# A float32 indexer on quarters of the array, a longer delay for the top-64, reordered split products and 512-wide last columns in a two-layer transformer trunk

## The chip, the core and the metric

The kernel runs on one core of a Trainium2 chip. The metric is the device time of one execution in microseconds. Engines by their names in the profile: PE is TensorE (matrix products and transposes; PEld is its weight load), DVE is VectorE, ACT is ScalarE, POOL is GpSimd, SP is SyncE, which issues most DMAs.

## What is computed

Two layers on 256 tokens of width 1024, all in float32. In each layer the normalised input is projected once (`w_in`) to seven groups of columns: queries, keys and values of two attentions a and b, and a small indexer (8 query heads of 32, one key head of 32, 8 weights).

```
h = rms_norm(x, g_mix); proj = h @ w_in           # qa ka va | iq ik iw | qb kb vb
dots  = einsum('bqhd,bsd->bqhs', iq, ik) * 32**-0.5
score = einsum('bqhs,bqh->bqs', relu(dots), iw * 8**-0.5)   # chunk-causal mask: chunks of 64
idx   = top_k(score, 64)                          # attention a sees these keys only
out_a = softmax(qa . ka[idx] * 64**-0.5) @ va[idx]          # 8 heads of 64
p     = softmax(qb . kb * 64**-0.5)                          # 4 heads, two maps each
out_b = rms_norm((p[0] - lam * p[1]) @ vb, g_subln) * (1 - lam_init)
x = x + concat(out_a, out_b) @ w_out
h2 = rms_norm(x, g_ffn)
x = x + (silu(h2 @ w_gate) * (h2 @ w_up)) @ w_down           # inner width 2816
```

After the second layer follows one more `rms_norm` with `g_final`. Queries iq, qa, qb and keys ik, ka, kb are turned by rotary angles first.

## The kernel before

Tokens lie in two blocks of 128 (b = 0, 1). Every large product is a split product: activation and weight are each cut into a high part, rounded to the format fp32r, and the rest, so that hi.whi + lo.whi + hi.wlo stands for one float32 product. `mm3` (L195 to L201) issues these three, lines L198, L199 and L200. Contraction runs over k in pieces of 128: 8 for the projections, gate and up, and wo, 22 for down. In one layer TensorE does, in this order, the projections idx, qb, kb, vb, qa, ka, va (2 blocks x 8 k x 3 products of up to 512 columns each), `wo` with the halves mixb (from attention b) and mixa, six column groups j of gate and up (the last one 256 wide), and `down`. In between stand the small works of rotary transposes (`ptq_`), the indexer (`ptx`, `dots`) and the attentions (`lg_` logits, `ppt_` transposed probabilities, `po` outputs).

Weights come in chunks of up to 1 MB by SP's queue into `wraw` (3 buffers). ScalarE rounds them to `whi` (L176), VectorE subtracts to get `wlo` (L177); both have 6 buffers. The first idx projection (L765) alone uses unsplit weights, since it opens the run; the split of its activations is done by `halved` in `startup`.

The indexer: after the rotary step `ixt` is repeated and split into `ixq` and `ixk`, four copies of 32 columns (hi, lo and again, so that one 128-row product contracts hi.hi, hi.lo, lo.hi and lo.lo); ScalarE writes the high parts (L396), VectorE the low ones (L397). Nine transposes per block (`ptx`) put them on partitions. `indexer` then issues eight fp32r products per block (`dots`, two heads per bank), ScalarE applies relu (L447), VectorE adds the weighted scores (L450), and finds the top 64 in eight rounds of MAX (L458) and MATCH_REPLACE (L460), ending in `amask` (L463).

The order on TensorE is written by `Weave`: the large products form the main thread, every other work is a thread that yields a due time (constants such as DIX, DG, DB) and is put between products once the modelled clock has come that far. The order on VectorE and ScalarE is set by the tile scheduler from the order of issue and a priority; the top-64 is issued `with tc.high_priority(offset=-LOWP)`, which puts it behind work issued up to LOWP instructions later.

Of the kernel before, what the change touches and what calls it, by code (L numbers as in the profile page):

```python
# [8 lines left out]
F32 = mybir.dt.float32  # L9
# [8 lines left out]
P = 128  # L18
D = 1024
S = 256  # L20
# [12 lines left out]
LOWP = 100  # L33
DG = 2.0
# [8 lines left out]
DIX = 13.0  # L43
# [66 lines left out]
def tile_hybrid_trunk(ctx, tc, x, xT, w_idx, w_in, w_out, w_gate, w_up, w_down, g_final, rope, out):  # L110
# [12 lines left out]
    NSUB = 1024  # L123
    chunks = []
# [6 lines left out]
    for L in range(DEPTH):  # L131
# [9 lines left out]
        for j in range(6):  # L141
            n = min(512, DFF - j * 512)
            step = 4 if n == 512 else 8
            for nm, w in (("gate", w_gate), ("up", w_up)):
                for a in range(0, KT, step):
                    c = add_chunk(w[L], range(a, a + step), j * 512, n)
                    for k in range(a, a + step):
                        plan[L, nm, j, k] = c
# [8 lines left out]
    def load(c):  # L157
        src, kts, c0, n = chunks[c]
        t = pool.tile([P, len(kts), n], F32, tag="wraw", bufs=3, name=f"wraw{c}")
        if n == NCOL["idx"]:  # L160
            for k in range(0, len(kts), 2):
                nc.sync.dma_start(t[:, k:k + 2], src[:, k:k + 2])
        else:
            nc.sync.dma_start(t, src[kts[0] * P:(kts[-1] + 1) * P, c0:c0 + n].rearrange("(k p) n -> p k n", p=P))
# [215 lines left out]
    def after_proj(L, nm, b, ps):  # L380
        name = f"{nm}{L}{b}"
        r = rstd["mix", L, b]
        if nm == "idx":
# [8 lines left out]
            sk = pool.tile([P, 1, 4, 32], F32R, tag="ixk", bufs=2, name=f"ixk{L}{b}")  # L392
            for st, hd, first, second in ((sq, slice(0, 8), slice(0, 4, 2), slice(1, 4, 2)),
                                          (sk, slice(8, 9), slice(0, 2), slice(2, 4))):
                src = t[:, hd].unsqueeze(2).to_broadcast([P, hd.stop - hd.start, 2, 32])
# [3 lines left out]
            iq = pool.tile([P, 8, P], F32R, tag="iqT", bufs=2, name=f"iqT{L}{b}")  # L399
            if b == 0:  # L400
                T["ik"] = pool.tile([P, S], F32R, tag="ikT", bufs=1, name=f"ikT{L}")
            flat = [v.bitcast(F32).rearrange("p h r d -> p h (r d)") for v in (sq, sk)]
            for g in range(2):
                pt = bank(f"ptx{L}{b}{g}").rearrange("p (k t) -> p k t", k=4)
                for k in range(4):
                    transpose(pt[:, k], flat[0][:, 4 * g + k])
                nc.scalar.copy(iq[:, 4 * g:4 * g + 4], pt)
            pt = bank(f"ptx{L}{b}2")
            transpose(pt[:, :P], flat[1][:, 0])
            nc.scalar.copy(T["ik"][:, b * P:(b + 1) * P], pt[:, :P])  # L410
            T["iq", b] = iq
# [441 lines left out]
```

## Time and profile before

| | |
|---|---|
| median of 3 runs (lowest to highest) | 640.1 us (640.01 to 640.23) |
| profiled execution | 640.0 us |
| its span | 638.2 us |
| PE busy | 628.1 us (98%) |
| PEld busy | 519.5 us (81%) |
| DVE busy | 434.9 us (68%) |
| ACT busy | 360.4 us (56%) |
| chain that ended last | PE 83%, DVE 11%, ACT 2%, issue 2%, DMA 2% |
| granted TensorE clock, tenths in 40 slices | 9 in all but the last, 8 |

The span runs from the first to the last instruction that the profile shows; the execution's own time is 1.8 us longer. Busy shares are averages over the run; by stretches they differ much, and the rows below tell them apart. TensorE's products overlap one another, so what one costs is read from the distance of two starts, not from its duration.

### The profile page before, as it was taken

The page shows a single profiled execution, that of the slowest core. Times are in us where ns is not written, and L with a number is a line of the kernel's source. Part 1 is how long each engine was busy: PE and PEld are TensorE (multiplying, and loading weights), DVE is VectorE, ACT ScalarE, POOL GpSimd, SP SyncE. Part 2 cuts the span into 40 slices and gives each one's busy share as a digit, 9 for nine tenths or more (in the row PEclk, how much of TensorE's full clock was granted, in tenths as well). Part 3 has the DMA queues.
Part 4 walks back from the last instruction along what each step waited for, and adds up shares of the span by engine and source line. Part 5 has one row for each costly group of instructions (what it writes and reads, how often), then busy time and mean ns, then how long its engine had stood idle before and what let it go on. Part 6 is the DMA issues. An engine that isn't in the chain of part 4 may idle for free.

```text
span 638.2 us, 8752 instructions
## 1 busy us (share of the span) xinstructions
PE 628.1 (98%) x3235; PEld 519.5 (81%) x3235; DVE 434.9 (68%) x922; ACT 360.4 (56%) x620; POOL 2.0 (0%) x12
## 2 busy tenths in 40 slices
PE   9999999999999999999999999999999999999996
PEld 5787787788888889888898787878888888898885
DVE  5999997696555456544598999876756555454445
ACT  4868677684454444433477767876744454443322
POOL 1000000000000000000000000000000000000000
PEclk9999999999999999999999999999999999999998
DMA  9873344346655555554277534323755655545611
GB/s 333 283 242 105 120 179 149 132 132 200 196 196 185 192 167 184 198 197 143 66 265 222 174 132 133 132 72 127 258 169 172 196 196 186 195 153 193 198 34 66
DMA packets 49307, 109.64 MB, mean 172 GB/s; under 512 B 1904, under 2 KB 6512, under 8 KB 49264
## 3 DMA queue, kind: packets, MB, share of 16 engines
q1 hardware_dynamic: 48256, 106.96, 50.2%
q10 hardware_dynamic: 1008, 2.12, 0.9%
q8 instruction: 25, 0.41, 0.3%
q14 instruction: 18, 0.15, 0.1%
HBM read 108.02 MB, written 1.05 MB: 171 GB/s over the span
## 4 chain that ended last, share of the span: by engine, by line
PE 83%; DVE 11%; ACT 2%; issue 2%; DMA 2%; ACTq 0%
PE ps_gate L198 6%; PE dn L199 6%; PE dn L198 6%; PE ps_gate L200 6%; PE dn L200 6%; PE ps_gate L199 6%; PE ps_up L200 6%; PE ps_up L198 6%; PE ps_up L199 6%; DVE wlo L177 3%; PE wo L199 2%; PE wo L200 2%; PE wo L198 2%; PE pth L204 2%; DVE topk L460 1%
## 5 line engine op out<-in xcount | busy, mean ns | idle before, releaser
L177 DVE TENSOR_TENSOR wlo<-wraw,whi 128x1024 fp32r<-128x1024 f32 (+1 forms) x200 | 241.5, 1213 | 139.1 <-ACT whi L176 134.5
L176 ACT CAST whi<-wraw 128x1024 fp32r<-128x1024 f32 (+1 forms) x200 | 206.7, 1043 | 153.5 <-PE dn L199 50.0
L198 PE MATMUL ps_gate<-whi,hi_ffn 128*128 128x512 f32 (+1 forms) x192 | 73.6, 383 | 0.0
L198 PE MATMUL dn<-whi,hi_ff 128*128 128x512 f32 (+1 forms) x198 | 73.1, 369 | 0.0
L199 PE MATMUL dn<-whi,lo_ff 128*128 128x512 f32 (+1 forms) x198 | 72.6, 367 | 0.0
L200 PE MATMUL dn<-wlo,hi_ff 128*128 128x512 f32 (+1 forms) x198 | 72.4, 366 | 0.0
L200 PE MATMUL ps_gate<-wlo,hi_ffn 128*128 128x512 f32 (+1 forms) x192 | 71.5, 373 | 0.0
L200 PE MATMUL ps_up<-wlo,hi_ffn 128*128 128x512 f32 (+1 forms) x192 | 71.3, 372 | 0.0
L199 PE MATMUL ps_gate<-whi,lo_ffn 128*128 128x512 f32 (+1 forms) x192 | 71.3, 371 | 0.0
L198 PE MATMUL ps_up<-whi,hi_ffn 128*128 128x512 f32 (+1 forms) x192 | 71.3, 371 | 0.0
L199 PE MATMUL ps_up<-whi,lo_ffn 128*128 128x512 f32 (+1 forms) x192 | 71.3, 371 | 0.0
L200 PEld LDWEIGHTS dn<-wlo,hi_ff 128*128 128x128 f32 x198 | 37.3, 188 | 6.2
L198 PEld LDWEIGHTS dn<-whi,hi_ff 128*128 128x128 f32 x198 | 37.4, 189 | 6.0
L199 PEld LDWEIGHTS dn<-whi,lo_ff 128*128 128x128 f32 x198 | 37.4, 189 | 5.8
L200 PEld LDWEIGHTS ps_gate<-wlo,hi_ffn 128*128 128x128 f32 x192 | 36.1, 188 | 6.6
L200 PEld LDWEIGHTS ps_up<-wlo,hi_ffn 128*128 128x128 f32 x192 | 36.2, 188 | 6.3
L199 PEld LDWEIGHTS ps_up<-whi,lo_ffn 128*128 128x128 f32 x192 | 36.2, 188 | 6.2
L198 PEld LDWEIGHTS ps_up<-whi,hi_ffn 128*128 128x128 f32 x192 | 36.2, 188 | 6.2
L199 PEld LDWEIGHTS ps_gate<-whi,lo_ffn 128*128 128x128 f32 x192 | 36.2, 189 | 5.6
L198 PEld LDWEIGHTS ps_gate<-whi,hi_ffn 128*128 128x128 f32 x192 | 36.2, 188 | 5.5
L302 ACT CAST hi_ff<-pth 128x512 fp32r<-128x512 f32 (+1 forms) x24 | 13.2, 549 | 19.9 <-PE pth L204 19.9
L303 DVE TENSOR_TENSOR lo_ff<-pth,hi_ff 128x512 fp32r<-128x512 f32 (+1 forms) x24 | 15.5, 645 | 8.8 <-ACT hi_ff L302 8.8
(324 smaller groups left out, 1035.4 us busy)
## 6 DMA issues: line engine op xcount, KB each, us to landing
wraw<-in_w_in_dram SPq DMA_DIRECT2D x24, 1024.0 KB, 5.1
wraw<-in_w_gate_dram SPq DMA_DIRECT2D x22, 1024.0 KB, 5.1
wraw<-in_w_up_dram SPq DMA_DIRECT2D x22, 1024.0 KB, 5.2
wraw<-in_w_down_dram SPq DMA_DIRECT2D x22, 1024.0 KB, 5.0
wraw<-in_w_out_dram SPq DMA_DIRECT2D x8, 1024.0 KB, 4.9
wraw<-in_w_idx_dram SPq DMA_DIRECT2D x8, 296.0 KB, 3.6
x<-in_x_dram SPq DMA_DIRECT2D x2, 512.0 KB, 7.9
xt<-in_xT_dram ACTq DMA_DIRECT2D x3, 256.0 KB, 6.2
```

Of the source, the lines that this page charges most:

```text
L176: nc.scalar.copy(hi, raw[c][:, s:s + step])
L177: nc.vector.tensor_tensor(lo, raw[c][:, s:s + step], hi.bitcast(F32), op=ALU.subtract)
L198: nc.tensor.matmul(ps, hi, whi, start=first, stop=False)
L199: nc.tensor.matmul(ps, lo, whi, start=False, stop=False)
L200: nc.tensor.matmul(ps, hi, wlo, start=False, stop=last)
L204: nc.tensor.transpose(o, i, ident)
L302: nc.scalar.copy(hi[:, :n], pt)
L303: nc.vector.tensor_tensor(lo[:, :n], pt, hi[:, :n].bitcast(F32), op=ALU.subtract)
L460: nc.vector.match_replace(out=nxt[:, :nk], in_to_replace=m8, in_values=cur[:, :nk], imm_value=TAKEN)
```

## The change

1. The indexer works in plain float32. `ixt` becomes 12 heads of 32 (8 queries, the key four times), written by two instructions; `ixq` and `ixk` are gone. Three transposes per block lay four heads on the four quarters of 32 rows. The dots are then 32-row products: head 4i + g uses rows 32g to 32g + 31, and the four g have a bank each. All eight products of a block are issued together, and the waits DG between them are gone.
2. LOWP goes from 100 to 300, DIX from 13 to 10.
3. `mm3` takes a list of outputs and issues hi.whi for all, then hi.wlo for all, then lo.whi for all. For mixb of wo and for all but the last six k of down, the list holds both halves of the columns; elsewhere it has one output.
4. The first layer's qb has an order of its own: per pair of k all products with whi of both blocks, then those with wlo; and in `startup` the second `halved(1, b)` stands ahead of `split_sub(2, 0)`.
5. The last 256 columns of gate and up share one 512-wide chunk ("both") and one bank per block. In the second layer's down, block 1's columns 512 to 1023 are one 512-wide product for all but the last six k.
6. The final norm adds up its parts as they come, one tile holds the output of a block.

```diff
-LOWP = 100
-DG = 2.0
+LOWP = 300
-DIX = 13.0
+DIX = 10.0
...
-    def mm3(ps, act, kt, w, first, last):
+    def mm3(outs, act, kt, first, last, second=False):
         hi, lo = act[kt]
-        whi, wlo = w
-        nc.tensor.matmul(ps, hi, whi, start=first, stop=False)
-        nc.tensor.matmul(ps, lo, whi, start=False, stop=False)
-        nc.tensor.matmul(ps, hi, wlo, start=False, stop=last)
-        W.spend(3 * max(0.107, 0.216 * ps.shape[-1] / 512))
+        for ps, whi, wlo in outs:
+            nc.tensor.matmul(ps, hi, whi, start=first, stop=False, skip_group_check=second)
+        for ps, whi, wlo in outs:
+            nc.tensor.matmul(ps, hi, wlo, start=False, stop=False, skip_group_check=second)
+        for ps, whi, wlo in outs:
+            nc.tensor.matmul(ps, lo, whi, start=False, stop=last, skip_group_check=second)
+            W.spend(3 * max(0.107, 0.216 * ps.shape[-1] / 512))
...
-            t = pool.tile([P, 9, 32], F32, tag="hff", bufs=3, name=f"ixt{L}{b}")
-            nc.vector.tensor_tensor(t.rearrange("p h d -> p (h d)"), a[:, :288], c[:, :288], op=ALU.add)
-            sq = pool.tile([P, 8, 4, 32], F32R, tag=("kbT", "kaT")[b], bufs=1, name=f"ixq{L}{b}")
...
-                nc.scalar.copy(st[:, :, first], src)
-                nc.vector.tensor_tensor(st[:, :, second], src, st[:, :, first].bitcast(F32), op=ALU.subtract)
+            t = pool.tile([P, 12, 32], F32, tag="hff", bufs=3, name=f"ixt{L}{b}")
+            keys = [v[:, 256:288].unsqueeze(1).to_broadcast([P, 4, 32]) for v in (a, c)]
+            nc.vector.tensor_tensor(t[:, :8].rearrange("p h d -> p (h d)"), a[:, :256], c[:, :256], op=ALU.add)
+            nc.vector.tensor_tensor(t[:, 8:], keys[0], keys[1], op=ALU.add)
             yield DIX, ()
...
+            for k in range(3):
+                transpose(pt[:, k], t[:, 4 * k:4 * k + 4].rearrange("p h d -> p (h d)"))
+            iq = T["iq", b] = pool.tile([P, 2, P], F32, tag="iqT", bufs=2, name=f"iqT{L}{b}")
...
+            banks = [bank(f"dots{L}{b}{g}").rearrange("p (i k) -> p i k", i=2) for g in range(4)]
+            for i in range(2):
+                for g in range(4):
+                    rws = slice(32 * g, 32 * g + 32)
+                    small_mm(0.054 * (b + 1), banks[g][:, i, :nk], T["iq", b][rws, i], T["ik"][rws, :nk],
+                             start=True, stop=True)
             first = True
             for g in range(4):
-                if g:
-                    yield DG, ()
...
+        if key == (0, "qb"):
+            for k0 in range(0, KT, 2):
...
+                for low in (False, True):
+                    for b in range(NB):
...
+                            if low:
+                                nc.tensor.matmul(ps, hi, wlo, start=False, stop=(k == KT - 1))
+                            else:
+                                nc.tensor.matmul(ps, hi, whi, start=(k == 0), stop=False)
+                                nc.tensor.matmul(ps, lo, whi, start=False, stop=False)
...
-                    for h in range(2):
-                        wo("mixb", 4, b, k, h)
+                    wo("mixb", 4, b, k, (0, 1))
...
+                    yield from group("ffn", L, (L, "both", j), 2 * n, False, after_both)
...
-                    for h in range(len(cuts[b])):
-                        down(b, h, kt)
+                    down(b, halves, kt)
...
-        nc.vector.tensor_reduce(v, ss[:, :n], axis=AX.X, op=ALU.add)
-        nc.scalar.activation(sd, v, AF.Sqrt, scale=1.0 / D, bias=eps)
+        nc.scalar.activation(sd, last, AF.Sqrt, scale=1.0 / D, bias=pre)
...
-            halved(1, 0)
+            for b in range(NB):
+                halved(1, b)
             split_sub(2, 0)
-            halved(1, 1)
             split_sub(2, 2)
```

How the order of instructions moves, at three places. In the rows stand line, operation, output and inputs; a trailing number such as _750 tells buffers of one name apart.

TensorE at the indexer's transposes of the first layer, before: they stand after fifteen products of kb, nine per block (`ixq_227` and `ixk_228` are block 0, `ixq_243` and `ixk_244` block 1).

```order
L200 MATMUL ps_kb_315<-wlo_0_276,hi_mix_142 128x512
L204 MATMUL ptx_350<-ident,ixq_227 128x128 x4
L204 MATMUL ptx_356<-ident,ixq_227 128x128 x4
L204 MATMUL ptx_362<-ident,ixk_228 128x128
L204 MATMUL ptx_366<-ident,ixq_243 128x128 x4
L204 MATMUL ptx_372<-ident,ixq_243 128x128 x4
L204 MATMUL ptx_378<-ident,ixk_244 128x128
L198 MATMUL ps_kb_315<-whi_0_275,hi_mix_142 128x512
```

The same place now (`ixt_225` is block 0, `ixt_236` block 1):

```order
L639 MATMUL ps_qb_211<-wlo_2_207,hi_mix_152 128x512 x2
L217 MATMUL ptx_295<-ident,ixt_225 128x128 x3
L217 MATMUL ptx_303<-ident,ixt_236 128x128 x3
L639 MATMUL ps_qb_212<-wlo_2_207,hi_mix_156 128x512 x2
L209 MATMUL ps_kb_312<-whi_0_265,hi_mix_132 128x512
```

Three per block are left, and they have moved ahead of the last two products of qb, which now read wlo.

VectorE ahead of the first `p_b` that is transposed in the first layer (`topk_531` and `m_006_533` are rounds of the top-64 of block 0; `wlo_0_782` is the split of a later weight), before:

```order
L460 MATCH_REPLACE topk_531<-m_005_529,topk_527 128x128
L458 MAX m_006_533<-topk_531 128x8
L177 TENSOR_TENSOR wlo_0_782<-wraw_586,whi_0_781 128x1024
L516 SCALAR_TENSOR_TENSOR p_b_615<-p_b_615,rc_b_622,p_b_624 128x128 x2
L489 RECIPROCAL rc_b_710<-sm_b_705 128x2
```

The same place now (`m_010_436`, `topk_438`, `m_011_440` and `topk_442` are rounds of block 1, 256 columns wide):

```order
L464 MATCH_REPLACE topk_403<-m_007_401,topk_399 128x128
L464 MATCH_REPLACE topk_438<-m_010_436,score_407 128x256
L467 TENSOR_SCALAR amask_405<-topk_403 128x128
L186 TENSOR_TENSOR wlo_0_749<-wraw_599,whi_0_748 128x1024
L493 RECIPROCAL rc_b_656<-sm_b_651 128x2
L462 MAX m_011_440<-topk_438 128x8
L517 TENSOR_SCALAR nl_658<-rc_b_656,neglam 128x2
...
L464 MATCH_REPLACE topk_442<-m_011_440,topk_438 128x256
L520 SCALAR_TENSOR_TENSOR p_b_640<-p_b_640,rc_b_647,p_b_649 128x128
L186 TENSOR_TENSOR wlo_2_753<-wraw_599,whi_2_752 128x1024
L520 SCALAR_TENSOR_TENSOR p_b_640<-p_b_640,rc_b_647,p_b_649 128x128
```

The last rounds of block 0, its mask, two rounds of block 1 and one more wlo now stand ahead of the second p_b instruction.

TensorE at the beginning of wo in the first layer (`hi_mb` and `lo_mb` are the parts of attention b's output, `wo_1228` and `wo_1229` the two halves of the columns), before:

```order
L198 MATMUL wo_1228<-whi_0_1075,hi_mb_1114 128x512
L199 MATMUL wo_1228<-whi_0_1075,lo_mb_1115 128x512
L200 MATMUL wo_1228<-wlo_0_1076,hi_mb_1114 128x512
L198 MATMUL wo_1229<-whi_0_1075,hi_mb_1114 128x512
L199 MATMUL wo_1229<-whi_0_1075,lo_mb_1115 128x512
L200 MATMUL wo_1229<-wlo_0_1076,hi_mb_1114 128x512
```

Now:

```order
L209 MATMUL wo_1205<-whi_0_1054,hi_mb_1145 128x512
L209 MATMUL wo_1206<-whi_0_1054,hi_mb_1145 128x512
L211 MATMUL wo_1205<-wlo_0_1055,hi_mb_1145 128x512
L211 MATMUL wo_1206<-wlo_0_1055,hi_mb_1145 128x512
L213 MATMUL wo_1205<-whi_0_1054,lo_mb_1146 128x512
L213 MATMUL wo_1206<-whi_0_1054,lo_mb_1146 128x512
```

The first product that reads `lo_mb` has moved from the second place to the fifth.

## Rows read from the trace of the kernel before

**Rows 1.** Busy time by stretch: us of busy time and instructions per engine, clock, DMA share.

```profile
21.00:90.00 69.00, 68.94 (x361) 56.19 (x362) 68.48 (x189) 51.38 (x107) 0.00 (x0) 1.00 0.52 175
90.00:330.00 240.00, 239.51 (x1228) 200.28 (x1227) 147.59 (x268) 129.11 (x210) 0.00 (x0) 1.00 0.52 172
330.00:365.00 35.00, 35.00 (x185) 28.98 (x185) 32.26 (x65) 25.17 (x44) 0.00 (x0) 1.00 0.60 193
```

**Rows 2.** What TensorE's weight loads waited for: us in all, times, longest.

```profile
PEld ppt_b L204 <- DVE p_b L516: 1.6, 2, 1.4
...
PEld ps_qb L200 <- DVE wlo L177: 1.3, 2, 0.7
...
PEld wo L199 <- DVE lo_ma L303: 1.1, 2, 0.5
...
PEld wo L199 <- DVE lo_mb L306: 1.0, 2, 0.5
...
PEld ptq_qb L204 <- DVE rp_qb L418: 0.5, 1, 0.5
```

**Rows 3.** TensorE in order of time, steady products: start, us, operation, tiles.

```profile
252.21 0.28 PE L198 MATMUL ps_up<-whi,hi_ffn 128*128 128x256 f32 x1
...
255.45 0.28 PE L198 MATMUL ps_up<-whi,hi_ffn 128*128 128x256 f32 x1
...
269.39 0.39 PE L198 MATMUL dn<-whi,hi_ff 128*128 128x512 f32 x1
...
270.98 0.39 PE L199 MATMUL dn<-whi,lo_ff 128*128 128x512 f32 x1
```

**Rows 4.** TensorE in order of time, small work between products.

```profile
49.42 0.39 PE L200 MATMUL ps_vb<-wlo,hi_mix 128*128 128x512 f32 x1
49.74 0.72 PE L431 MATMUL lg_b<-kbT,qb00T 64*128 64x128 f32 x8
50.38 0.66 PE L204 MATMUL ptq_kb<-ident,rp_kb 128*128 128x128 f32 x4
50.80 0.48 PE L431 MATMUL dots<-ikT,iqT 128*128 128x256 f32 x2
51.12 0.40 PE L198 MATMUL ps_vb<-whi,hi_mix 128*128 128x512 f32 x1
...
67.80 1.14 PE L431 MATMUL lg_b<-kbT,qb01T 64*128 64x256 f32 x8
68.86 0.44 PE L204 MATMUL ppt_b<-ident,p_b 128*128 128x128 f32 x2
```

**Rows 5.** VectorE and TensorE in order of time, the first 27 us.

```profile
12.92 1.23 DVE L177 TENSOR_TENSOR wlo<-wraw,whi 128x1024 fp32r<-128x1024 f32 x1 [1.94 <-ACT whi L176]
...
24.98 0.69 DVE L397 TENSOR_TENSOR ixq<-ixt,ixq 128x512 fp32r<-128x512 f32 x1
...
25.59 0.22 DVE L397 TENSOR_TENSOR ixk<-ixt,ixk 128x64 fp32r<-128x64 f32 x1
...
25.72 0.45 DVE L389 TENSOR_TENSOR ixt<-rp_idx,rp_idx 128x288 f32<-128x288 f32 x1
...
26.09 1.22 DVE L177 TENSOR_TENSOR wlo<-wraw,whi 128x1024 fp32r<-128x1024 f32 x1
26.13 0.39 PE L198 MATMUL ps_kb<-whi,hi_mix 128*128 128x512 f32 x1
```

**Rows 6.** VectorE and TensorE in order of time, around the first ppt_b.

```profile
58.02 0.61 DVE L516 SCALAR_TENSOR_TENSOR p_b<-p_b,rc_b,p_b 128x128 f32<-128x128 f32 x2
...
59.50 0.38 PE L204 MATMUL ppt_b<-ident,p_b 128*128 128x128 f32 x2
...
62.17 0.43 DVE L458 MAX8 m<-topk 128x8 f32<-128x256 f32 x1
...
63.04 1.22 DVE L177 TENSOR_TENSOR wlo<-wraw,whi 128x1024 fp32r<-128x1024 f32 x1
```

**Rows 7.** VectorE in the last 6 us.

```profile
632.83 0.16 DVE L732 TENSOR_REDUCE v_fin<-ss_fin 128x1 f32<-128x3 f32 x1
```

More of the change, by code (lines that the diff above doesn't have):

```diff
@@ L123, in tile_hybrid_trunk @@
     NSUB = 1024
+    LASTN = DFF % 512
     chunks = []
@@ L141, in tile_hybrid_trunk @@
         for j in range(6):
[L142 to L148, printed above, removed]
+            if DFF - j * 512 >= 512:
+                for nm, w in (("gate", w_gate), ("up", w_up)):
+                    for a in range(0, KT, 4):
+                        c = add_chunk(w[L], range(a, a + 4), j * 512, 512)
+                        for k in range(a, a + 4):
+                            plan[L, nm, j, k] = c
+            else:
+                for a in range(0, KT, 4):
+                    c = add_chunk((w_gate[L], w_up[L]), range(a, a + 4), j * 512, 2 * LASTN)
+                    for k in range(a, a + 4):
+                        plan[L, "both", j, k] = c
         for a in range(0, DFF // P, 2):
@@ L408, in after_proj @@
[L408 to L411, printed above, removed]
+                T["ik"] = pool.tile([P, S], F32, tag="ikT", bufs=1, name=f"ikT{L}")
+            nc.scalar.copy(T["ik"][:, b * P:(b + 1) * P], pt[:, 2])
+            nc.scalar.copy(iq, pt[:, :2])
         elif nm in ("va", "vb"):
@@ L438, in indexer @@
             sc = pool.tile([P, S], F32, tag="score", bufs=2, name=f"score{L}{b}")
+            banks = [bank(f"dots{L}{b}{g}").rearrange("p (i k) -> p i k", i=2) for g in range(4)]
[4 more added lines that the diff above has]
+                             start=True, stop=True)
             first = True
             for g in range(4):
[L441 to L443 removed]
+                rl = pool.tile([P, 2, S], F32, tag="relu", bufs=2, name=f"relu{L}{b}{g}")
+                nc.scalar.activation(rl[:, :, :nk], banks[g][:, :, :nk], AF.Relu, scale=32 ** -0.5)
                 for i in range(2):
[L445 to L449 removed]
+                    h = 4 * i + g
                     nc.vector.scalar_tensor_tensor(sc[:, :nk], rl[:, i, :nk], T["iw", b][:, h:h + 1],
@@ L621, in group @@
         banks = [bank(f"ps_{key[1]}{L}{key[2] if len(key) > 2 else ''}{b}") for b in range(NB)]
+        if key == (0, "qb"):
+            for k0 in range(0, KT, 2):
+                c = plan[key + (k0,)]
+                ensure(c)
+                for low in (False, True):
+                    for b in range(NB):
+                        yield 0, (("act", kind, L, b, k0 // 4),)
+                        for k in (k0, k0 + 1):
+                            hi, lo = acts[kind, L, b][k]
+                            whi, wlo = parts[c, k]
+                            ps = banks[b][:, :n]
+                            if low:
+                                nc.tensor.matmul(ps, hi, wlo, start=False, stop=(k == KT - 1))
+                            else:
+                                nc.tensor.matmul(ps, hi, whi, start=(k == 0), stop=False)
+                                nc.tensor.matmul(ps, lo, whi, start=False, stop=False)
+                            W.spend(0.227 * (1 if low else 2))
+            for b in range(NB):
+                after(b, banks[b])
+            return
         halves = (0, 1)
@@ L720, in final @@
         ss = small(4, f"ss_fin{b}")
-        xg = []
+        pre, sd, half, y0, t, r = (small(1, f"{w}_fin{b}") for w in ("pre", "sd", "half", "y0", "t", "r"))
+        o = pool.tile([P, D], F32, tag="whi", bufs=6, name=f"fo{b}")
         for i, (a, e) in enumerate(cuts):
@@ L783, in startup @@
             scale(3)
-            halved(1, 0)
+            for b in range(NB):
+                halved(1, b)
             split_sub(2, 0)
-            halved(1, 1)
             split_sub(2, 2)
```

88 lines of the change are left out of this document (43 added, 45 removed).

## The prediction

> **What bounds the kernel now.** I read the busy times of the page first, then busy time by stretch, then the waits in front of TensorE, then single instructions of TensorE and VectorE in order of time. TensorE is busy for 628.1 of 638.2 us, so only two things can shorten the run: less TensorE work, or fewer of its waits. From 21 to 90 us, the first layer's projections, VectorE is as full as TensorE: 68.48 of 69 us [rows 1]. There a wait of TensorE on VectorE is repaid only by a shorter VectorE list. In the second layer VectorE has some air: 32.26 of 35 us between 330 and 365. The waits of TensorE's loads that the change touches are those for p_b (1.6 us), wlo in ps_qb (1.3), lo_ma and lo_mb in wo (1.1 and 1.0) and rp_qb (0.5) [rows 2]. A split product starts 0.227 us after the last when 512 wide (269.39 to 270.98, 7 steps), 0.120 when 256 wide (252.21 to 255.45, 27 steps) [rows 3]: the narrow one costs 0.013 us more per pair.
>
> **The indexer's transposes.** 18 transposes per layer become 6. Four take 0.42 us (50.38 to 50.80) [rows 4], so 24 fewer give 24 x 0.105 = -2.5 us.
>
> **The indexer's dots.** Before, two took 0.32 us with an entry of about 0.09, so 0.23; 16 pairs are 3.7 us, 1.85 per layer. No row shows 32-row float32 products; the nearest are lg_b, 64 rows, two at a time. Eight records (four products of 128 columns) take 0.64 us (49.74 to 50.38) and at 256 columns 1.06 (67.80 to 68.86) [rows 4]; the difference, 0.42, is what four of 128 columns cost, and 0.22 is fixed. Per layer there are now eight of 128 and eight of 256 columns. Two at a time they take 0.84 + 1.68 + 0.22 = 2.74 us, four at a time 1.48, one at a time 5.26. Against 1.85 this is +1.8, -0.7 and +6.8 us for both layers. I take four at a time, since the two groups of lg_b do overlap fully, and -0.4 for both layers, as the second layer has two such stretches. The Trainium skill ("TensorE: Matmul & The Clock Gate", Part 3, Measured speedup vs the span model) gives 3.07 times, not 4, for four row tiles; by that the 1.26 us of the products would be 1.64, and the sum 0.8 us higher, inside the bounds above. No run here shows it yet.
>
> **Changes of TensorE's mode.** Entering lg_b from a product takes 0.32 us instead of 0.227 (49.42 to 49.74) [rows 4]; an entry or a return costs about 0.09. In the new order there are seven more returns from transposes to products and six more entries or exits of row-tiled products: 13 x 0.09 = +1.2 us. The Trainium skill ("TensorEngine Tiling (Array Packing)", Key Properties) says that changing the tiling mode, not just the tile, drains TensorE. That rule speaks against the change; the 0.09 us agrees with it and already contains the drain, so the sum stays.
>
> **512-wide ends.** The last gate and up columns: 96 x 0.120 - 48 x 0.227 = 0.62 us per layer, 1.25 for two. The second layer's down for rows 128 to 255: 16 x 3 steps at 0.013 = 0.62. Together -1.9 us. That loads and splits have other shapes there costs nothing: VectorE and ScalarE are far from full in these stretches, 147.59 and 129.11 of the 240 us between 90 and 330 [rows 1]. If that cover went, TensorE would wait for a wlo of 1.14 us.
>
> TensorE's work: -2.5 - 0.4 + 1.2 - 1.9 = **-3.6 us**.
>
> **Waits that go.** At the start the hi.wlo products of qb move behind eight that need only whi, and the two wlo come earlier, as the second half of the activation split fits into VectorE's idle 1.94 us before 12.92 [rows 5]. The wait in ps_qb was 0.5 us on the products and 1.3 on their loads [rows 2], with a slow step behind each; I take -1.0. ptq_qb's wait: -0.3 of 0.5. In wo the lo product comes fifth (mixb, two halves) or third (mixa, one half) instead of second, so 0.68 or 0.23 us later. That covers the 0.5 of lo_mb and half of the 0.55 of lo_ma, each twice: -1.0 and -0.5. The 1.6 us at ppt_b are almost all one pair of the second layer (longest 1.4); with the third p_b no longer behind as much work, -1.2. Sum **-4.0 us**.
>
> **Waits that come.** (1) ptx of the second block. ScalarE's and VectorE's splits ixq (0.61) and ixk (0.13) go, but ixt is now two instructions, an estimated 0.34 + 0.20 instead of 0.37 from row 25.72. Before, ixt ended at 26.09 [rows 5]; now 26.09 - 0.74 + 2 x 0.17 = 25.7. A wlo of 1.14 us stands ahead of it in VectorE's list. TensorE asks for it two products before the end of ps_qb: 26.13 - 1.0 - 2 x 0.227 + 0.3 for three transposes = 25.0. So +0.8 us (0.4 to 1.1); behind it stand the last two qb products and all of kb.
> (2) The first ppt_b. In the new list all of block 0's top-64, two rounds of block 1's and one more wlo stand ahead of the second L520 (p_b): two MATCH and one MAX of 128 columns, two MATCH and two MAX of 256, amask and wlo. A round over 256 costs 0.87 us (62.17 to 63.04) [rows 6], two 1.74; one and a half of 128 columns and amask I estimate at 0.7, somewhat over half as much per round; wlo 1.14: 3.6. Less the splits, 2 x 0.74 - 0.34 = 1.14, this is +2.4 on a VectorE that never idles, so p_b, which was there at 58.6 (58.02 + 0.61), comes at 61.0. TensorE arrives at 59.50 + 9 more qa products (2.04) - 12 transposes (1.26) - dots 0.35 - starts 1.3 + ptx 0.8 = 59.4. So +1.6 us (0.8 to 2.5), with every qa and ka product queued behind.
> (3) Later pairs of the first layer: two to three more wlo stand ahead of p_b, partly balanced by the products moved ahead on TensorE; +0.3 (0 to 1).
> (4) The second layer's first ppt_b. Eight rounds of block 1, and two wlo more, less 1.14: 7.0 + 2.3 - 1.14 = 8.1 us. VectorE idles 2.7 us in 330 to 365 [rows 1] and the scores come earlier with the dots. Between 0 and 8.1 - 2.7 = 5.4; I take 0.8, near the lower end, because these rounds fill idle time rather than push anything until the list is full.
> Sum **+3.5 us**.
>
> **Tail.** The reduction of the three partial sums, 0.16 us [rows 7] and its step, goes: -0.2.
>
> **Sum.** -3.6 - 4.0 + 3.5 - 0.2 = -4.3. The profiled execution took 640.0 us, its span 638.2 plus 1.8 outside; the median of the runs is 640.1. So **635.7 us**.
>
> **Rivals.**
> *No new waits* (chance 0.14): if p_b and ixt come in time, 635.7 - 3.5 = 632.2. For it: VectorE's list is 1.14 us shorter per layer. Against: it is full to 99% in the first layer [rows 1].
> *The second layer's top-64 is not absorbed* (0.11): 5.4 instead of 0.8 at its first ppt_b, 640.3, no change that can be told. For it: 8.1 us are put ahead of p_b. Against: the idle 2.7 us and the earlier dots.
> *Dots one at a time* (0.07), the slower side: the 32-row products neither overlap nor hide their weight loads; place: the dots of both layers; price 5.26 instead of 1.48 per layer, +7.2 against my term, so 642.9. It makes the kernel slower from about 3.6 us per layer on. For it: each has its own load, and the array is regrouped. Against: lg_b's pairs [rows 4]. Two at a time is 637.9, within my forecast's range.
> *Same stationary operand skips its load* (0.03): two products in a row now share the activation's hi. If this saved what a step has above 512 columns at 2.4 GHz, 0.227 - 0.213 us, on some 1000 products, 14 us, the time would be 622. Against: dn already has consecutive products with the same hi, and its step is 0.227 as elsewhere [rows 3].
> *The reordering of products does nothing for wo* (inside the forecast): 1.5 us less gain, 637.2.
>
> **Chances and range.** Forecast 0.63 (own range 634 to 637.9), the rivals as given, 0.02 for anything else. A change of under 0.2%, 1.3 us, can't be told from none. Faster than 638.8: nearly all of the forecast, the first and fourth rivals: 0.80. Within 0.2%: the second rival and the forecast's upper edge, 0.12. Slower: 0.08. The range takes in the first rival's time and what lies between the forecast and the second: 632.0 to 639.4.
>
> **What would show it.** TensorE's busy time falls by 3 to 4 us. dots: sixteen products in about 1.5 us per layer, four starting nearly together; 5 us refutes it. ps_qb waits for no wlo; ptx of block 1 waits about 0.8 us on ixt. ppt_b of the first layer waits 1 to 2 us on p_b, which starts after 60 us. The second layer's long wait at ppt_b, 1.4 us, is gone. In wo, lo_mb waits for nothing. ps_both shows 48 products per layer, 0.227 us apart. The forecast is wrong if the waits at ppt_b together pass 5 us, or if the dots take more than 3.6 us per layer.

## The result, and the profile after

The changed kernel took 646.4 us (median of 4 runs, 645.6 to 647.4) against 640.1 for the kernel before in the same job: a ratio of 1.0097, interval 1.0085 to 1.0109. The forecast was 635.7, a gain of 4.3 us; it is a loss of 6.4, and above the range. The profiled execution has a span of 645.2 us, against 638.2. Of the four runs two took 645.6 and 645.8 us at a mean granted clock of 0.997 and two 647.1 and 647.4 us at 0.994, and the profiled one is the 647.1.

The page of the changed kernel: busy time by engine, the clock in 40 slices, and the chain that ended last.

```profile
PE 626.7 (97%) x3099; PEld 509.3 (79%) x3099; DVE 437.0 (68%) x921; ACT 353.7 (55%) x608; POOL 2.0 (0%) x12
...
PEclk9999999899999999999999999999999999999998
...
PE 74%; DVE 17%; ACT 5%; issue 2%; DVEq 0%; ACTq 0%
```

TensorE is busy for 1.4 us less than before while the span is 7.0 us longer, so it idles 8.4 us more. On the chain, PE has fallen from 83% to 74%, and DVE and ACT have risen from 13% together to 22%. Slice 8, about 113 to 129 us, is at a lower clock.

What TensorE waited for in the changed kernel (us in all, times, longest), which answers to [rows 2]; here for its products and transposes, so the numbers are somewhat smaller than those of the loads:

```profile
PE ppt_b L217 <- DVE p_b L520: 4.0, 3, 2.6
PE wo L209 <- ACT hi_mb L318: 2.4, 2, 1.2
PE lg_a L434 <- ACT kaT L375: 1.5, 1, 1.5
...
PE wo L213 <- DVE lo_mb L319: 0.8, 2, 0.4
PE ptx L217 <- DVE ixt L403: 0.7, 1, 0.7
```

ps_qb's wait for wlo and ptq_qb's are gone, as forecast. ptx's wait is there with 0.7 us for the forecast 0.8. But ppt_b has 4.0 us, and hi_mb and kaT, which the forecast didn't have at all, 3.9.

Where the time went, by the starts of the first product of each kind on TensorE (us; for comparison the two best experiments, told below):

| stretch | before | after | e12 | e15 |
|---|---|---|---|---|
| up to the first qb | 13.9 | 13.5 | 13.2 | 13.8 |
| qb to wo, layer 1 | 85.7 | 88.5 | 86.8 | 84.4 |
| wo to gate | 32.8 | 35.7 | 32.1 | 32.8 |
| gate to the second layer's idx | 187.3 | 186.8 | 186.8 | 186.8 |
| idx to wo, layer 2 | 92.1 | 93.3 | 92.1 | 92.9 |
| wo to gate | 32.8 | 33.9 | 32.1 | 32.1 |
| gate to the last product | 187.0 | 186.3 | 186.7 | 186.3 |
| behind its start | 6.6 | 7.2 | 6.9 | 7.4 |

Gate, up and down gain 1.2 us in all. The projections and wo lose 8.0, which is where attentions and top-64 stand. The first row says nothing of the change: e10 runs the same instructions as before up to there and takes 13.1 us.

**The first ppt_b.** VectorE and TensorE of the changed kernel in order of time, layer 1, which answers to [rows 6]:

```profile
57.70 0.22 DVE L467 TENSOR_SCALAR amask<-topk 128x128 f32<-128x128 f32 x1
57.83 1.22 DVE L186 TENSOR_TENSOR wlo<-wraw,whi 128x1024 fp32r<-128x1024 f32 x1
...
60.30 0.34 DVE L520 SCALAR_TENSOR_TENSOR p_b<-p_b,rc_b,p_b 128x128 f32<-128x128 f32 x1
60.56 1.22 DVE L186 TENSOR_TENSOR wlo<-wraw,whi 128x1024 fp32r<-128x1024 f32 x1
60.70 0.33 PE L217 MATMUL ppt_b<-ident,p_b 128*128 128x128 f32 x1 [0.35 <-DVE p_b L520]
61.70 0.34 DVE L520 SCALAR_TENSOR_TENSOR p_b<-p_b,rc_b,p_b 128x128 f32<-128x128 f32 x1
62.09 0.33 PE L217 MATMUL ppt_b<-ident,p_b 128*128 128x128 f32 x1 [1.07 <-DVE p_b L520]
```

p_b starts 2.3 and 3.7 us later than the 58.02 of before, block 0's mask and two wlo ahead of it, and TensorE waits 0.35 + 1.07 = 1.4 us. The second layer, the same view:

```profile
365.95 0.22 DVE L467 TENSOR_SCALAR amask<-topk 128x128 f32<-128x128 f32 x1
...
377.63 0.29 DVE L467 TENSOR_SCALAR amask<-topk 128x256 f32<-128x256 f32 x1
377.83 1.22 DVE L186 TENSOR_TENSOR wlo<-wraw,whi 128x1024 fp32r<-128x1024 f32 x1
378.97 0.61 DVE L520 SCALAR_TENSOR_TENSOR p_b<-p_b,rc_b,p_b 128x128 f32<-128x128 f32 x2
379.37 0.59 PE L217 MATMUL ppt_b<-ident,p_b 128*128 128x128 f32 x2 [2.62 <-DVE p_b L520]
```

Here the eight rounds (all but the first MAX) and the mask of block 1, 256 columns wide, stand between block 0's mask and p_b. Nothing needs that mask before block 1's logits of attention a (lg_a at 420.83); TensorE stands still for 2.62 us for it. In the kernel before, p_b stood ahead of those rounds and was ready 1.6 us before TensorE asked for it:

```profile
368.75 0.61 DVE L516 SCALAR_TENSOR_TENSOR p_b<-p_b,rc_b,p_b 128x128 f32<-128x128 f32 x2
...
371.03 0.38 PE L204 MATMUL ppt_b<-ident,p_b 128*128 128x128 f32 x2
```

By stretch, VectorE of the changed kernel (the first two answer to [rows 1]):

```profile
21.00:90.00 69.00, 66.78 (x357) 52.85 (x357) 67.78 (x184) 45.87 (x97) 0.00 (x0) 1.00 0.53 174
330.00:365.00 35.00, 35.00 (x191) 28.48 (x191) 34.28 (x84) 22.68 (x35) 0.00 (x0) 1.00 0.56 190
340.00:379.00 39.00, 36.49 (x200) 28.45 (x198) 38.01 (x107) 24.39 (x47) 0.00 (x0) 1.00 0.45 150
90.00:136.00 46.00, 42.91 (x255) 33.68 (x254) 31.33 (x106) 30.17 (x79) 0.00 (x0) 0.96 0.34 115
```

From 340 to 379 us, up to p_b, it is 38.01 of 39 us busy: no idle time is left for these rounds. From 90 to 136 it is busy for only 31.33 us; in the kernel before, for 36.14:

```profile
90.00:136.00 46.00, 45.51 (x279) 36.49 (x278) 36.14 (x115) 34.42 (x85) 0.00 (x0) 1.00 0.36 121
```

The top-64 was work for a later stretch with room, and is now done early in a stretch that has none.

**wo.** TensorE at block 1's part, first layer of the changed kernel:

```profile
110.41 0.66 PE L217 MATMUL pt_mb<-ident,on 128*128 128x128 f32 x4
110.82 0.71 PE L209 MATMUL wo<-whi,hi_mb 128*128 128x512 f32 x2
111.36 0.63 PE L211 MATMUL wo<-wlo,hi_mb 128*128 128x512 f32 x2
111.83 0.63 PE L213 MATMUL wo<-whi,lo_mb 128*128 128x512 f32 x2
113.65 0.74 PE L209 MATMUL wo<-whi,hi_mb 128*128 128x512 f32 x2 [1.20 <-ACT hi_mb L318]
...
115.24 0.96 PE L213 MATMUL wo<-whi,lo_mb 128*128 128x512 f32 x2 [0.37 <-DVE lo_mb L319]
...
116.70 1.20 PE L209 MATMUL wo<-whi,hi_mb 128*128 128x512 f32 x2
117.70 1.05 PE L211 MATMUL wo<-wlo,hi_mb 128*128 128x512 f32 x2
```

Only six products, the last of block 0, stand between block 1's transposes pt_mb and the first product that reads hi_mb; before, four lg_a and eight po (two records each) stood there as well:

```profile
107.09 0.60 PE L204 MATMUL pt_mb<-ident,on 128*128 128x128 f32 x4
107.62 1.13 PE L431 MATMUL lg_a<-kaT,qa01T 64*128 64x256 f32 x8
108.69 1.09 PE L431 MATMUL po<-pT_a,va 128*64 128x128 f32 x16
109.71 0.50 PE L198 MATMUL wo<-whi,hi_mb 128*128 128x512 f32 x1
```

In the changed kernel ScalarE begins hi_mb at 112.93, behind steps of attention a (p_a and hi_ma) that stand ahead of it in its list, and so TensorE waits, 1.20 and 0.37 us. After that its steps are 0.5 instead of 0.23 us:

```profile
112.00:114.00 2.00, 0.80 (x4) 0.32 (x4) 1.73 (x9) 1.92 (x6) 0.00 (x0) 1.00 0.00 0
...
116.00:119.00 3.00, 3.00 (x11) 2.52 (x10) 1.22 (x1) 1.53 (x2) 0.00 (x0) 0.50 0.00 0
```

The granted clock is 0.50, that is 1.2 GHz, from 116 to 119; TensorE had been busy for 0.80 of the 2 us from 112 and for 1.63 of the 2 us from 114. From 116.00 to 119.22 stand four transposes and six products, about 1.9 us at the full clock, so some 1.3 us are lost on top of the wait. In the second layer the same two waits (1.22 us up to 429.21, 0.39 up to 430.79) are followed by no such fall.

**The end.** VectorE and TensorE of the changed kernel, which answers to [rows 7]:

```profile
635.82 0.39 PE L209 MATMUL dn<-whi,hi_ff 128*128 128x256 f32 x1 [0.52 <-DVE x L746]
...
637.76 1.02 DVE L763 TENSOR_TENSOR fo<-x,gfin 128x512 f32<-128x512 f32 x2
637.96 0.28 PE L213 MATMUL dn<-whi,lo_ff 128*128 128x256 f32 x1
...
638.76 0.41 DVE L746 TENSOR_TENSOR x<-dn,x 128x256 f32<-128x256 f32 x1
```

The reduction is gone, but two 512-wide multiplications stand ahead of the last addition to x, which starts 0.80 us after the start of the last product; before, it was 0.31 (631.59 to 631.90). The first row is a wait that the kernel before doesn't have: the last 256 columns of block 1 share a bank with the 256 before them, and TensorE waits 0.52 us until VectorE has added those to x.

### The profile page after: what moved, and what is told of

It is laid out like the page before. It is cut to its first block, busy times and chain, and to the rows that moved or that the text cites. A ratio compares the mean times of both kernels' runs of the same rounds, so it can differ in the third digit from the quotient of the medians.

```text
span 645.2 us, 8394 instructions
## 1 busy us (share of the span) xinstructions
PE 626.7 (97%) x3099; PEld 509.3 (79%) x3099; DVE 437.0 (68%) x921; ACT 353.7 (55%) x608; POOL 2.0 (0%) x12
## 4 chain that ended last, share of the span: by engine, by line
PE 74%; DVE 17%; ACT 5%; issue 2%; DVEq 0%; ACTq 0%
PE dn L209 6%; PE dn L211 6%; PE dn L213 6%; PE ps_gate L209 6%; PE ps_gate L213 6%; PE ps_gate L211 6%; PE ps_up L213 6%; PE ps_up L211 6%; PE ps_up L209 6%; DVE wlo L186 6%; PE wo L213 2%; ACT p_a L490 2%; DVE score L454 2%; PE wo L209 2%; PE wo L211 2%
## 5 line engine op out<-in xcount | busy, mean ns | idle before, releaser
L209 PE MATMUL ps_gate<-whi,hi_ffn 128*128 128x512 f32 x160 | 64.3, 402 | 0.0
L213 PE MATMUL ps_gate<-whi,lo_ffn 128*128 128x512 f32 x160 | 62.5, 391 | 0.0
L211 PE MATMUL ps_gate<-wlo,hi_ffn 128*128 128x512 f32 x160 | 62.3, 389 | 0.0
L213 PE MATMUL ps_up<-whi,lo_ffn 128*128 128x512 f32 x160 | 62.3, 389 | 0.0
L209 PE MATMUL ps_up<-whi,hi_ffn 128*128 128x512 f32 x160 | 62.2, 389 | 0.0
L211 PE MATMUL ps_up<-wlo,hi_ffn 128*128 128x512 f32 x160 | 62.2, 389 | 0.0
L209 PE MATMUL dn<-whi,hi_ff 128*128 128x512 f32 (+1 forms) x182 | 59.9, 386 | 0.5 <-DVE x L746 0.5
L213 PE MATMUL dn<-whi,lo_ff 128*128 128x512 f32 (+1 forms) x182 | 59.2, 382 | 0.0
L211 PE MATMUL dn<-wlo,hi_ff 128*128 128x512 f32 (+1 forms) x182 | 59.2, 382 | 0.0
L209 PEld LDWEIGHTS dn<-whi,hi_ff 128*128 128x128 f32 x182 | 33.9, 188 | 7.0 <-DVE x L746 0.7
L315 ACT CAST hi_ff<-pth 128x512 fp32r<-128x512 f32 (+1 forms) x24 | 13.1, 547 | 21.0 <-PE pth L217 21.0
L490 ACT ACTIVATE p_b<-p_b,mx_b 128x128 f32<-128x128 f32 (+1 forms) x32 | 14.4, 452 | 18.7 <-DVE mx_b L487 18.6
```

What stands on the lines that cost most here:

```text
L209: nc.tensor.matmul(ps, hi, whi, start=first, stop=False, skip_group_check=second)
L211: nc.tensor.matmul(ps, hi, wlo, start=False, stop=False, skip_group_check=second)
L213: nc.tensor.matmul(ps, lo, whi, start=False, stop=last, skip_group_check=second)
L315: nc.scalar.copy(hi[:, :n], pt)
L490: nc.scalar.activation(p[:, i, :nk], p[:, i, :nk], AF.Exp, scale=-1.0, bias=mx[:, i:i + 1], accum_out=sm[:, i:i + 1])
```

## The experiments

The theory: the loss is order. All scores of a block come at once and early, the scheduler puts the top-64 that hangs on them ahead of p_b in VectorE's list, and TensorE, whose order is fixed too, waits. Rivals: the new order of the split products costs; the float32 indexer is dearer in itself. The expectations name their theories by letters; behind each it is said in words what the run decided. Unless another is named, an edit is one to the changed kernel. Ratios are to the kernel before, run on the same chip.

**e1: everything but the indexer.** The old indexer with its 18 transposes and fp32r dots, LOWP = 100, DG = 2.0, DIX = 13.0.

> The changed kernel with the indexer of before (fp32r dots, nine transposes per block, LOWP 100, DG 2, DIX 13); the other parts of the change stay. Theory A (the indexer part delays attention b: TensorE waits at ppt_b, lg_a and wo): most waits at ppt_b (5.1 us on the loads) and hi_mb (3.3) are gone and the first ppt_b of layer 1 starts before 60 us; 634 to 637 us. Theory B (the reordered split products and the longer runs of products without small work cost it): 643 to 647 us, with the wait of wo on hi_mb still there.

Measured: 639.0 us, ratio 0.9982 (0.9973 to 0.9992), 2 us above the range of theory A and far from that of B. The waits at kaT, at hi_mb and at the first ppt_b of both layers are gone; a later ppt_b of each layer waits 1.0 us. Against 646.4, the indexer costs 7.4 us here; the rest of the change gains 1.1.

**e2: the indexer alone.** The kernel before with the float32 indexer, LOWP = 300, DIX = 10.0.

> The kernel before with only the float32 indexer, LOWP 300 and DIX 10. Theory A: it carries the loss, 645 to 650 us, with waits of about 1.8 us at the first layer's and 2.9 us at the second layer's first ppt_b. Theory B: no such loss, 637 to 641 us.

Measured: 650.7 us, 1.0173 (1.0156 to 1.0190), just above the range. Waits as in the changed kernel: ppt_b 2.5 (in the second layer alone; the 1.8 expected in the first didn't come), hi_mb 2.3, kaT 2.2, lo_mb 2.2 us. Both ways of dividing the change put the loss in the indexer with its LOWP and DIX, 7.4 us in one and 10.6 in the other.

**e3: half the top-64.** It leaves out four of the eight rounds, so another selection results.

```diff
-                for it in range(TOPK // 8):
+                for it in range(TOPK // 16):
```

> The changed kernel with four instead of eight rounds of the top-64 per block (it takes 32 keys, so the result differs); TensorE's order is the same row for row. Theory A1 (VectorE's list, with the top-64 ahead of p_b, is what makes attention b late): some 5 us per layer leave VectorE, the waits at the first ppt_b of both layers (1.8 and 2.9 us) fall under 0.5, kaT and hi_mb come earlier too; 636 to 641 us. Theory A2 (TensorE's and ScalarE's own order makes them late, VectorE's load is not decisive): 645 to 647 us, hi_mb's wait stays at 3.3 us.

Measured: 640.4 us, 1.0009 (1.0000 to 1.0018): 6.0 us less than with all rounds. Its waits:

```profile
PE wo L209 <- ACT hi_mb L318: 2.4, 2, 1.2
...
PE ppt_b L217 <- DVE p_b L520: 0.8, 1, 0.8
```

ppt_b falls from 4.0 to 0.8 and kaT to 0.2; hi_mb stays at 2.4 and so isn't the doing of the rounds that were cut.

**e10: the same cut in the kernel before**, to see what the rounds cost there. The result differs in the same way.

> The kernel before with four instead of eight rounds of the top-64 per block (32 keys, so the result differs). Theory C: there the top-64 mostly fills time that VectorE would wait, so the same cut that gave the changed kernel 6.0 us gives little, 0.5 to 2.5 us: 637.5 to 639.5. Rival (VectorE's load as such is the bound, wherever the top-64 stands): again about 6 us, 633 to 635.

Measured: 638.6 us, 0.9974 (0.9964 to 0.9984), 1.7 us less. The same instructions taken away give 6.0 us in one kernel and 1.7 in the other: what they cost is their place in the list.

**e4: the old order within a split product** (hi.whi, lo.whi, hi.wlo, one half after the other).

```diff
-        for ps, whi, wlo in outs:
-            nc.tensor.matmul(ps, hi, wlo, start=False, stop=False, skip_group_check=second)
-        for ps, whi, wlo in outs:
-            nc.tensor.matmul(ps, lo, whi, start=False, stop=last, skip_group_check=second)
+            nc.tensor.matmul(ps, lo, whi, start=False, stop=False, skip_group_check=second)
+            nc.tensor.matmul(ps, hi, wlo, start=False, stop=last, skip_group_check=second)
```

> The changed kernel with the order of before inside each split product (hi.whi, lo.whi, hi.wlo, one half of the columns after the other). Theory A: the wait for hi_mb stays, lo_mb and lo_ma are waited for earlier again, about +1 to +2 us on the changed kernel's 646.4: 647 to 649. Theory B (the new order of products costs it): 640 to 644.

Measured: 649.9 us, 1.0151 (1.0134 to 1.0168), a little above the range of theory A. The new order is worth 3.5 us here; lo_mb's wait is 2.2 instead of 0.8. The rival that blames part 3 falls.

**e5, e6, e7, e8: moving due times a little.** e5 holds back the dots, e6 brings attention b's later steps forward, e7 does both, e8 is e7 with the old final norm.

```diff
+            yield (8.0, 10.0)[b], ()     # e5, ahead of the dots
...
-DB = (8.0, 10.0)
+DB = (6.0, 8.0)                          # e6
```

> The changed kernel with the float32 dots of block 0 issued 8 modelled us later and those of block 1 another 10 later, about where before had them; on VectorE p_b then stands ahead of the last rounds of block 0's top-64, and in the second layer ahead of block 1's. Theory A1 (the early scores fill VectorE's list ahead of p_b): the waits at the first ppt_b (1.8 and 2.9 us) fall under 0.5 each, hi_mb's wait in wo stays; 640 to 643 us. Rival (it is not the early scores): 645 to 648, with the same waits.

> The changed kernel with DB 6 and 8 instead of 8 and 10: TensorE's small work of attention b is due 2 modelled us earlier, so that two lg_a groups and po stand again between the last pt_mb and the first product of wo that reads it. Theory A2 (TensorE's order puts pt_mb too close to wo): the waits on hi_mb and lo_mb (3.3 and 1.6 us on the loads) and the stretch at the lower clock near 116 us go, 641 to 643 us; the wait at the first ppt_b grows by what ppt_b comes earlier, since p_b's time is VectorE's. Rival (attention b is late for VectorE alone): pt_mb waits instead, 645 to 647.

> Both of the last two edits. If A1 and A2 are two separate causes their gains add: 636 to 638 us, with no wait over 1 us at ppt_b, kaT or hi_mb. If they are one, it is no better than the better of the two, 640 to 642.

> As the last one, with the final norm of before. The changed kernel's tail is 0.6 us longer from the last product to the end (7.2 us against 6.6), since 512-wide fo steps stand ahead of the last x on VectorE; so 0.5 to 0.7 us less than the run with both edits. Rival: the tail's length does not depend on this, no difference.

Measured: 647.8 (ratio 1.0117), 649.1 (1.0142), 647.8 (1.0121) and 648.1 us (1.0126), all with intervals of 0.0019 or less to each side: none gains, and e5, e6 and e7 miss what their theories forecast. In e5 the first layer's wait at the first ppt_b goes (p_b at 53.9 us, ppt_b at 57.8), the second's stays at 2.6, since there block 0's rounds and block 1's first five still stand ahead of p_b; pt_mb and hi_mb wait 2.8 together. In e6 the waits at hi_mb and lo_mb go and both stretches from wo to gate take 32.9 us, but the later steps now come to ppt_b too early:

```profile
PE ppt_b L217 <- DVE p_b L520: 8.1, 3, 4.7
```

A due time that frees one wait passes it on to the next as long as VectorE's list stays as it is. The old final norm (e8 against e7) makes no difference that can be measured.

**e9, e11: two heads at a time.** The float32 products on 32 rows, but two heads, DG, two heads, as before; LOWP = 100, DIX = 13.0. e11 has the old final norm too.

```diff
+                if g:
+                    yield DG, ()
...
+                for i in range(2):
+                    small_mm(0.107 * (b + 1), ps[:, i, :nk], T["iq", b][rws, i], T["ik"][rws, :nk],
+                             start=True, stop=True)
```

> The changed kernel with its float32 dots on 32 rows, but issued two heads at a time with the waits DG 2 between them, DIX 13 and LOWP 100, as before had its dots. Theory C (the moment of issue makes the loss, not the form of the indexer: all scores at once bring the top-64 ahead of p_b and leave VectorE without filling work later): 636 to 639 us, the first ppt_b at about 59 us with a wait under 1, VectorE busier between 90 and 136 us than the changed kernel's 31.3. Rival (the form itself, 32 rows and fewer transposes): 644 to 647.

> As the run with spread dots, with the final norm of before: 0.5 to 0.7 us less, if the longer tail of the changed kernel comes from the order of its fo steps; otherwise the same.

Measured: 644.7 us, 1.0070 (1.0055 to 1.0085), and 644.8, 1.0070 (1.0054 to 1.0087). The waits at ppt_b, kaT and hi_mb are all gone and both stretches from wo to gate take 32.1 us, yet the time misses the expected 636 to 639 and lies in the rival's range. The dots account for it: two heads of one bank lie on the same quarter of the rows.

```profile
31.14 0.71 PE L435 MATMUL dots<-ikT,iqT 32*128 32x128 f32 x4
31.78 0.50 PE L210 MATMUL ps_kb<-whi,hi_mix 128*128 128x512 f32 x1
```

Two products of 128 columns (two records each) take 0.64 us here; in e15 eight on four quarters take 0.66 (41.46 to 42.12). Over a layer it is 6.15 us against 1.7 to 2.3, some 8 us over both layers, so this run traded a loss by waits for one by work and didn't tell whether order is everything.

**e12: two parts alone.** The kernel before with the reordered split products and the 512-wide ends.

> The kernel before with two parts alone: the reordered split products and the 512-wide ends; indexer, first-layer qb, startup and final norm as before. By my terms of TensorE's work, 512-wide ends -1.9 and wo -1.5: 636.5 to 637.5 us; if the two parts are worth only what the run with the old indexer showed (-1.1 for these and the rest), 638 to 639.

Measured: 638.4 us, 0.9971 (0.9959 to 0.9983), 1 to 2 us above what my terms give and inside the second range: each stretch from wo to gate gains 0.7 us and gate, up and down 0.8 in all, but ps_qb still waits 1.3 us for wlo, and the first layer's wo starts at 100.0 instead of 99.6.

**e13, e14: the dots much later.** The dots stay four at a time and are held back so far that p_b stands ahead of the top-64 in both layers. e14 has DB = (6.0, 8.0) and DSUB = (14.0, 5.0) as well, all attention b earlier.

```diff
+            yield (12.0, 16.0)[b], ()     # ahead of the dots
```

> The changed kernel with one more line: ahead of the dots block b waits until 12 or 16 us on the modelled clock, instead of at once. In VectorE's list p_b then stands ahead of block 0's top-64 in the first layer and ahead of block 1's in the second, and wo of block 1 has lg_a and po between it and its transposes again. Theory C (the order of VectorE's list is the loss): the waits at ppt_b and hi_mb fall below 1 us together, the clock's mean returns to 0.997, and the time is 637 to 640. Theory D (the float32 indexer is dearer in itself, by its dots, its banks or the holes it leaves): the time stays above 643. Between the two: the late top-64 of block 1 makes a new wait at lg_a or ppt_a, and the time is 640 to 643.

> The same with attention b's later steps 2 us earlier on the modelled clock. Theory C: what is left of the hi_mb wait goes, 0.5 to 1.5 us faster than without. Theory D: nothing gained, or ppt_b waits come as they did when attention b was moved earlier alone: 0 to 4 us slower.

Measured: e13 643.1 us, 1.0039 (1.0026 to 1.0052); e14 648.2, 1.0113 (1.0096 to 1.0131). By their times both speak for theory D: e13 is above 643, and e14 is 5.1 us slower than e13, more than even D's 4. The waits speak otherwise. In e13 no wait at ppt_b or hi_mb is left, as the theory of order has it, but one took their place, in the first layer at block 1's pt_mb:

```profile
PE pt_mb L217 <- ACT on L556: 2.8, 1, 2.8
```

e14, with attention b earlier, brought ppt_b's back (5.1 us) and left 2.3 at pt_mb.

**e15: e13, and pt_mb behind work that is ready.**

```diff
-        yield DSUB[b], ()
+        yield DSUB[b] + (3.0 if L == 0 and b else 0.0), ()
```

> e13 with one more number: in the first layer block 1's pt_mb (after the inner norm of attention b) is due 3 us later on the modelled clock. On TensorE it then stands behind all products of wo with block 0's mixb and behind lg_a and ppt_a, instead of six products ahead of them. It is aimed at the one long wait that e13 has left, 2.8 us at pt_mb on the norm. Theory C (all that the changed kernel loses is order): most of the 2.8 goes, and the time is 639.5 to 641.5, no slower than before by more than 0.2%. Theory D (VectorE's list of the first layer decides, wherever TensorE waits): the wait comes back behind pt_mb, at hi_mb or lo_mb, and the time stays at 642.5 to 643.5.

Measured: 638.5 us (median of 10, 638.3 to 638.8), 0.9974 (0.9965 to 0.9983), 1 us below the range of theory C. TensorE at block 1's part of wo in this kernel:

```profile
104.12 1.13 PE L434 MATMUL lg_a<-kaT,qa01T 64*128 64x256 f32 x8
...
106.36 0.65 PE L217 MATMUL pt_mb<-ident,on 128*128 128x128 f32 x4 [0.52 <-ACT on L556]
106.95 1.13 PE L434 MATMUL lg_a<-kaT,qa01T 64*128 64x256 f32 x8
108.01 1.09 PE L434 MATMUL po<-pT_a,va 128*64 128x128 f32 x16
109.04 0.73 PE L209 MATMUL wo<-whi,hi_mb 128*128 128x512 f32 x2
```

lg_a and po cover hi_mb, as they did before the change, and the wait for the norm has fallen from 2.8 to 0.5 us. In the second layer p_b comes in time, ahead of block 1's rounds:

```profile
366.39 0.61 DVE L521 SCALAR_TENSOR_TENSOR p_b<-p_b,rc_b,p_b 128x128 f32<-128x128 f32 x2
...
368.04 0.44 PE L217 MATMUL ppt_b<-ident,p_b 128*128 128x128 f32 x2
...
376.90 0.42 DVE L463 MAX8 m<-score 128x8 f32<-128x256 f32 x1
```

Two edits of due times, with no instruction taken away or made faster, give 7.9 us. That is more than the indexer's whole cost in e1 (7.4). So the loss is order, and the rival that the indexer is dearer in itself falls. e15 and e12 beat both kernels, and can't be told from each other: in this order the float32 indexer costs nothing, and gains nothing either. e15 keeps LOWP at 300 and DIX at 10, so these two by themselves don't make the loss; no run changes only one of them.

## Why the prediction was wrong, step by step

**TensorE's work, -3.6: right in kind, too large.** The steps at ptx, without its wait, fell from 1.9 and 1.8 us in the two layers to 0.8 and 0.5; 1.25 less was forecast for each. The dots take 2.3 us in the first layer, where both blocks come as one burst of 32 records and the second's loads wait 0.8 us for relu to free banks, and 1.7 in the second; 1.48 was forecast, 1.9 and 1.8 it was before. (By its own terms, -0.7 and 0.22 for a second stretch, the forecast's -0.4 should have been -0.5.) Of slow first steps, about 0.1 us over the usual, there are some 67 in projections and wo instead of 56, 1.3 us more in all, for a forecast 1.2. The Trainium skill ("TensorEngine Tiling (Array Packing)", Key Properties) has a change of tiling mode drain the array. A step of that size stands behind the row-tiled products, but also behind transposes on the whole array, where no tiling changes (0.31 us from 371.17 to 371.48 in the kernel before), so these steps don't show that a drain makes them. The 512-wide ends gained 1.2 of 1.9: 0.5 in the first layer, where 0.62 was forecast, and 0.7 in the second, where 1.24 was; there dn's new wait on x takes 0.52 us back. Together the work fell by some 2.0 us, and PE's busy time by 1.4, where 3 to 4 was to be seen.

**The start, -1.0, and wait (1), +0.8: right in place, but not on the path.** Block 1's ptx waits 0.7 us, and kb starts at 26.29 as against 26.13, though six transposes and this wait now stand ahead of it; without them it would be over a us earlier. In e1, with the new start and the old indexer, kb begins at 24.8 us, but vb at 41.4 (before 41.3) and va at 84.2 (83.1). The prediction itself says that VectorE is full there, and that a wait comes back only by a shorter list; it then booked the gain in full.

**wo, -1.5: the step failed.** The products were put right, and with enough work behind pt_mb the step is worth what was said, 0.7 us per layer in e12; in the changed kernel the new order of all split products is worth 3.5 (e4). What failed is the place of pt_mb: in block 1 it slipped past lg_a and po to six products ahead of its use. e1 and e2 put this in the indexer's part. The likely reason is that due times count modelled work, and the small work on TensorE's clock became less, so that threads come due more products later; no run shows this alone. TensorE then waits 2.4 us for hi_mb and 0.8 for lo_mb, where before it waited 0.3 for lo_mb. The order on record showed wo's products but was not read for what stands between pt_mb and them.

**Wait (2), the first ppt_b, +1.6: right**, with 1.4 us and p_b after 60 us. **Wait (3), later pairs of the first layer, +0.3: none came** at ppt_b.

**Wait (4), the second layer's, +0.8: failed, and the longest wait that came.** It is 2.6 us, 3.0 at the loads. The upper bound, a rough sum, held to the tenth: p_b starts at 378.97 instead of 368.75, 10.2 us later, and the layer itself 4.8 (324.5 against 319.7), so VectorE's list has made it 5.4 us later, which is 8.1 - 2.7. What failed is the reason for taking 0.8, that the rounds fill idle time: the 2.7 us that there are were already in the bound. What was to be taken off is the slack that p_b had before, from its end at 369.4 to ppt_b at 371.0, and the 0.8 us that TensorE came later; 5.4 - 1.6 - 0.8 is 3.0.

**Not in the list at all:** kaT, 1.5 us, and the late chain behind it, since each late p_b moves the rest of attention b on VectorE and ScalarE; and the clock after the waits in wo, some 1.3 us in the profiled execution. The listed terms as they came, by a rough sum, make some 640 to 641 us, already past the upper end of the range; hi_mb and lo_mb (2.9 more than before), kaT and the clock carry it on to 646 to 647. The rival "not absorbed" had the right mechanism, but put 5.4 us at the first ppt_b, where 2.6 came, and stopped there, so it came to 640.3 and not 646.4.

**The tail, -0.2: the other way,** +0.6. A reduction of 0.16 us was counted, and the multiplications ahead of the last addition weren't. e12, with the 512-wide ends and the old norm, stands at +0.3, so each has about half of it. The new norm gives its half back: with the old one (e11) dn's wait on x is 0.9 instead of 0.5 us (e9) and the tail 0.4 shorter, and the times are the same (644.8 and 644.7).

"Dots one at a time" and "same stationary operand" were refuted as expected: 1.7 to 2.3 us per layer, and steps of 0.23. What the forecast said would refute it did so in part: ppt_b's loads wait 5.1 us together, just above the 5.

Read against e15, the forecast's gain was too high even without the waits that come. e15 gains 1.7 us, not 7.8: TensorE waits for other things (ptq_ka 1.3, ob 0.7, ptx 0.5, pt_mb 0.5 us), and the rounds of block 1, now later, may again stand ahead of something; that was not shown. How much of it a better order could still give wasn't tried.

## What to carry to other kernels

Where one engine's order is fixed by a scheduler, work that gets ready earlier is not free: it goes into the list ahead of what is needed sooner, and the next engine waits, then the one behind it. Read what stands between a producer and its consumer on both engines, for every pair that the change shifts, and charge added work against the idle time that is really there up to that point; what is left over is the wait. A small kernel saving can also shift every due time that is counted in modelled work, so move those with it.

## What the runs showed of the hardware

Products of 32 rows overlap when they lie on different quarters and don't on one: two on one quarter take 0.64 us at 128 columns and 1.06 at 256 (e9), eight on four quarters 0.66 and 1.08 (e15). With the fixed 0.22 us per stretch taken off, as in the prediction, eight would take 1.68 and 3.36 us on one quarter against 0.44 and 0.86 on four, 3.8 to 3.9 times. In e9 a pair of block 0 and the next pair, of block 1 and on another quarter, are issued together once, and take 1.07 us, as long as the second alone. The Trainium skill ("TensorE: Matmul & The Clock Gate", Part 3, Measured speedup vs the span model) has 3.07 for four row tiles at 512 columns. At 128 and 256 columns these runs show more. Each quarter has a bank of its own here and a pair shares one, so no run tells the quarter from the bank.

A wait can cost more than its own length, and not each time. The granted clock fell to 0.50 for some 3 us in the changed kernel after two waits in a row of 1.2 and 0.4 us, with TensorE busy in 0.80 and 1.63 of two times 2 us; the same waits in its second layer, the 2.62 us at ppt_b there and the 2.8 us at pt_mb in e13's profiled execution brought no fall. It also differs from one execution of a kernel to the next: the runs of the changed kernel at a mean clock of 0.997 and 0.994 lie some 1.5 us apart, and those of e13 took 641.7 and 642.0 us at 0.998, 643.1 to 643.8 at 0.995.
